# A state-space scan's forward pass, taken apart into steps, with the tensor engine's order through it written by hand

## The chip, the cores and the metric

The kernel runs on one core of one Trainium2 chip. The metric is the device time in microseconds (us) of one execution. TensorE (PE) does matrix products, VectorE (DVE), ScalarE (ACT) and GpSimd (POOL) do the elementwise work, SyncE (SP) issues nearly all transfers (DMA).

## The reference, cut to what matters

Two layers run over 1024 latent and 256 context tokens (1280 in all) with 1024 channels. The change lies in the even layer: a bidirectional state-space scan (16 heads of 64 channels in 2 groups, state of 128, chunks of 128 tokens) beside a convolution branch, and one output projection over both. For one direction the reference computes

```python
def ssd_chunked(x, dt, a, bm, cm, h0):
    ...
    y_diag = jnp.einsum('btlgn,btsgn,btlsgr->...', cc, bc, decay) @ xdt   # within a chunk
    states = jnp.einsum('btsgn,btsgr,btsgrp->btgrpn', bc, decay_to_end, xdt)
    ...  # h_in: state entering each chunk, by a scan over chunks
    y_off = jnp.einsum('btlgn,btgrpn,btlgr->btlgrp', cc, h_in, jnp.exp(a_cum))
    return y_diag + y_off
```

(the first line is drawn together from two). Both directions are summed with a skip term, gated by silu(z), normalised (RMS) and give the scan's half of the concatenation that the output projection `w_out` multiplies. The other half, the convolution's, is multiplied by the lower half of `w_out`.

## The kernel before

Before the stage of the change, the input projections, the convolution branch and the backward pass over the states (`ssd_back`) are done, and their results lie in DRAM. The stage (in `layer0`, inside `with ExitStack() as e3`) does three things side by side over ten chunks, or token tiles, of 128 tokens:

- The scan, class `SsdFwd`, one object `S[c]` for each chunk. `prep` loads the chunk (`xt`, `bcT`, the rows `rst` that `rows` is cast from), scales x on POOL (`tmp`, L1488), makes the forward state `Hf` for the next chunk (two products, L1495, each in a bank `ms`, added on DVE at L1499), the product of C and B (L1508) and the diagonal's coefficients. `mix` makes the output in four quarters (g, j) of four heads each: two products with 15 rows give the exponents (L1553, banks `sg0` and `sg1`, called the pair below), DVE merges them (L1556), ACT takes the exponential (`dec`, L1558), POOL multiplies by C^T B (L1559), and 8 small products of two records each (L1563) add up the diagonal part in bank `yd`. The parts that come from the states entering the chunk are four products, one for each group and direction (L1542, bank `m2`), each scaled and added on DVE (L1545, L1546). `finish` gates with z (L1570), takes the RMS statistic and transposes (L1578) into `wt_d`.
- `stage_b`, for each token tile the convolution's half of the output projection: 48 products (L1009) of 512 columns in two banks `m0` and `m1`, called the filler below, with their input loaded and split (`yl`, L997, L157, L158), then a gate and the residual (L1042, L1043).
- 16 columns of the next layer's modulation (`mod_chan`, L207 to L213): for each, two halves of weights (`mr`, one buffer, L1134) are loaded, cast on ACT and split on DVE (`mh`, `ml`, two buffers), multiplied in 16 small products, copied, and turned by a last product (L212). They use the banks of the filler (`mm`).

Nothing in this stage is ordered by hand: the program's order gives priorities, and the framework's scheduler orders each engine's instructions ahead of the run by its own estimate of times. On the chip each engine follows that order. Behind the stage, `stage_a` multiplies the scan's half by the upper half of `w_out` (also L1009), with weights split into the buffers of the lower half (L961, L962). The attention of the second layer already runs in a block whose TensorE order is written by hand.

Two banks carry the tag `ms`: states, C^T B, transposes and row broadcasts share them.

Of the kernel before, what the change touches and what calls it, by code (L numbers as in the profile page):

```python
# [7 lines left out]
F32 = mybir.dt.float32  # L8
# [81 lines left out]
def run(steps):  # L90
    """Emit a sequence that is emitted in steps."""
    for _ in steps:
        pass
# [6 lines left out]
# What is done on the tensor engine beside the attention, in this order: projections of queries (q) and gates (g) of a group's  # L100
# two head pairs, both halves of the output projection by token tile (c, d) and their weights (R, W, V); @n: from the n-th unit on.
# [4 lines left out]
# Columns of it for each key tile, by unit of the attention.  # L106
BESIDE = (2944,) * 10 + (3840,) * 6


class Kern:  # L110
# [78 lines left out]
    def mod_chan_(self, layer, m, dst, pool, plus=0.0, halves=1, bank="mm", ahead=None, raw=None, parts=None):  # L189
        """Columns m*128.. of the modulation, channel-major [P, 2] (latents, context)."""  # L190
# [24 lines left out]
    def gate_rows(self, layer, j, dst, bank="ms"):  # L215
        """Gate of one stream broadcast over partitions, [P, D]."""
# [8 lines left out]
    def layer0(self):  # L225
# [63 lines left out]
        with ExitStack() as e3:  # L289
# [12 lines left out]
            self.stage_b(2, ob, w, yb_d, tb_d, grow, y0)  # L302
            S[0].prep()
            for c in range(NT):
                S[c].mix()
                if c < NT - 1:
                    S[c + 1].prep()
                S[c].finish()
                if c < NT - 1:
                    self.stage_b((c + 3) % NT, ob, w, yb_d, tb_d, grow)  # L310
                for _ in range(2):
                    if mods:
                        m, d, plus = mods.pop(0)
                        self.mod_chan(1, m, d, mp, plus=plus, halves=2, ahead=ahead)
                        if not mods:
                            em.close()
                            wl3 = ea.enter_context(self.pool(name="wl3", bufs=1))
                            for k in range(4, 6):
                                wa.append((k, wl3.tile([P, D], F32, name=f"wa{k}", tag=f"wa{k}"), (wl3, f"wa{k}")))
                                nc.sync.dma_start(wa[k][1], A["wout0"][k])  # L320
                if c == 4:
                    for k in range(4):
                        nc.vector.tensor_copy(wa[k][1][:1, :1], self.Hf[:1, :1])
                        nc.sync.dma_start(wa[k][1], A["wout0"][k])
# [42 lines left out]
    def layer1(self, h1, va_d, e0, free_h1):  # L367
# [56 lines left out]
    def rope(self, q, ps, a, b, out):  # L424
        """Rotated queries or keys of two heads (128 channels), latents a..b."""
# [65 lines left out]
    def attention(self, wp, W, hhi, hlo, kf_d, va_d, yc_d, gd_d, yd_d, den_d, rd_d, sk_d, ew, free_h1):  # L491
        tc, nc, A = self.tc, self.nc, self.A
        LS = SLICES[:2]
        with ExitStack() as e:
# [44 lines left out]
            def fill(kv):  # L539
                """Stationary forms of one group's keys and values."""  # L540
# [20 lines left out]
            def rest():  # L561
                """What fills the tensor engine beside the attention, with the columns of each step; None while there is nothing to do."""
# [98 lines left out]
    def att_max(self, kv, s, qf, KV, out, u, sk_d):  # L661
        """Stationary-side queries of 2 blocks and the shift of each row."""
# [58 lines left out]
    def att_s(self, KV, mv, b, x, kb, off):  # L721
        """Exponentials of the scores of one key tile, 4 heads, split."""
# [32 lines left out]
    def out1_open(self, yc_d, wr, raws):  # L755
        """Pools and first half of the last output weight."""
# [9 lines left out]
    def out1_c(self, o, t):  # L766
        """The latent stream's residual plus the gated-MLP half of the output projection."""
# [15 lines left out]
    def out1_den(self, q, den_d, rd_d, sk_d, s, h0=0, h1=16):  # L783
        """Reciprocals of twice the softmax denominators, sinks included, of a quarter of the queries, heads h0..h1."""
# [12 lines left out]
    def out1_next(self, o, qp, wr):  # L797
        """Second half of the last output weight."""
# [10 lines left out]
    def out1_y(self, o, q, yd_d, gd_d, rd_d, t0, n, k0, k1, eng):  # L809
        """Gated attention of tokens t0..t0+n (within a quarter), channel tiles k0..k1, split."""  # L810
# [23 lines left out]
    def out1_mm(self, ps, y, w, f, ks, a=0, i0=0):  # L834
        """Channel tiles ks of the product for one half of the channels."""
# [7 lines left out]
    def out1_ln(self, o, x, ps, t):  # L843
        """Residual and the last layer norm."""
# [23 lines left out]
    def out1_d(self, o, q, ten, t, y0):  # L868
        """The attention's half of the output projection of one token tile."""
# [15 lines left out]
    def out1_d67(self, o, q, ten):  # L885
        """The last quarter: the last group's channels come last."""
# [20 lines left out]
    def conformer(self, cv, csum, e):  # L907
        """silu(layer norm over channels) of the convolution, in place."""
# [38 lines left out]
    def split_wo(self, wo, raws, slots, vec=None):  # L947
        """Split one half of an output weight; low parts go to free slots and to those of the values loaded for the tiles before."""
# [17 lines left out]
    def load_wo(self, wo, wr, src, pool_lo=(), more=(), raws=()):  # L966
        """One half (8 K tiles) of an output weight, split; raws are loaded already, the next ones land in the slots of more."""
# [19 lines left out]
    def out_mm(self, ob, src, w, parts=None, by_k=False):  # L987
        """Token tile of an output projection half: two PSUM banks."""
# [23 lines left out]
    def ln_mv(self, q, t):  # L1012
        """mean and rstd over the free dimension."""
# [586 lines left out]
```

## Time and profile before

| | us |
|---|---|
| median of 3 runs | 2266.37 |
| lowest and highest | 2262.7 and 2266.95 |
| span of the profiled execution | 2267.6 |
| PE busy in it | 2148.1 (95%) |
| DVE / ACT / POOL busy | 1470.1 / 1005.1 / 1015.7 |

For the profiled execution no other time than its span is given. The span is read from the first to the last instruction. A matmul's end is modelled, so that a busy PE is not one at its peak; gaps between starts tell more. PEclk is the granted clock as a share of 2.4 GHz; 0.5 is the lower of its two levels, 1.2 GHz. A matmul of plain 32-bit operands leaves two records in the trace.

### The profile page before, as it was taken

The numbers are of one execution on the slowest core, as the hardware profiler recorded it, in microseconds if no ns is written. First come the engines' busy times: TensorE is split into PE (matmuls) and PEld (weight loads), VectorE is DVE, ScalarE is ACT, GpSimd is POOL, SyncE is SP. The second block draws the span as 40 slices with busy tenths as digits, with TensorE's granted clock in tenths as the row PEclk, the third lists the DMA queues.
The fourth block names the chain that finished last, engine by engine and source line by source line (L and its number), as shares of the span: only waits on it lengthen the run. The fifth ranks groups of instructions, "written<-read, shape, count | busy, mean of one in ns | idle before, by whom it ended". The sixth has DMA issues, their size and how long they took to land.

```text
span 2267.6 us, 28582 instructions
## 1 busy us (share of the span) xinstructions
PE 2148.1 (95%) x10748; PEld 1647.3 (73%) x10748; DVE 1470.1 (65%) x1912; ACT 1005.1 (44%) x1553; POOL 1015.7 (45%) x652
## 2 busy tenths in 40 slices
PE   7998998889999999999999999999999999899997
PEld 6877876769997766656789788888666666666676
DVE  6799999988743377677775133223665566566677
ACT  4355565543552233333333233325556666545510
POOL 0088998870223355444330128433344444424453
PEclk9999999989999999899999999999999999899998
DMA  7121111115535765555434224323112111523363
GB/s 271 57 67 57 42 51 64 63 59 170 180 113 191 249 194 176 169 192 180 140 115 134 75 77 170 128 84 98 51 45 60 31 45 53 161 83 116 111 187 128
DMA packets 160145, 262.79 MB, mean 116 GB/s; under 512 B 19028, under 2 KB 98768, under 8 KB 159752
## 3 DMA queue, kind: packets, MB, share of 16 engines
q1 hardware_dynamic: 158584, 257.45, 34.9%
q0 software_dynamic: 1280, 3.26, 0.5%
q8 instruction: 84, 1.38, 0.2%
q14 instruction: 53, 0.43, 0.1%
q10 hardware_dynamic: 144, 0.26, 0.0%
HBM read 186.55 MB, written 74.32 MB: 115 GB/s over the span
## 4 chain that ended last, share of the span: by engine, by line
PE 58%; DVE 7%; DMA 5%; ACT 3%; issue 2%; POOL 2%; SPq 0%; POOLq 0%; DVEq 0%; ACTq 0%
PE m L170 28%; PE m L1009 12%; PE po L746 4%; PE st L728 2%; PE st L729 1%; PE ms L691 1%; DMA mr<-in_modw_dram 1%; PE m L840 1%; PE po L1542 1%; DVE ml L158 1%; PE ms L686 1%; ACT rb L433 1%; POOL ks L828 1%; PE m L691 1%; PE yd L1563 1%
## 5 line engine op out<-in xcount | busy, mean ns | idle before, releaser
L170 PE MATMUL m<-hhi,wh 128*128 128x512 f32 (+1 forms) x840 | 306.9, 369 | 36.8 <-ACT pad L1235 35.2
L1216 POOL TENSOR_TENSOR accq<-accq,prod 128x1295 f32<-128x1295 f32 x90 | 319.0, 3545 | 43.7 <-ACT prod L1215 30.3
L170 PE MATMUL m<-hlo,wh 128*128 128x512 f32 (+1 forms) x840 | 308.2, 367 | 0.0
L170 PE MATMUL m<-hhi,wl 128*128 128x512 f32 (+1 forms) x840 | 306.1, 365 | 1.0 <-DVE wl L158 1.0
L1224 DVE SCALAR_TENSOR_TENSOR acc<-u,vwh,acc 128x1295 f32<-128x1295 f32 x150 | 234.8, 1565 | 6.1 <-issue 2.2
L739 POOL TENSOR_TENSOR pl<-pt,ph 128x512 fp32r<-128x512 f32 x96 | 129.0, 1344 | 236.7 <-ACT ph L738 227.7
L170 PE MATMUL m<-h1hi,wh 128*128 128x512 f32 (+1 forms) x544 | 218.3, 401 | 2.0 <-ACT rb L433 1.4
L170 PE MATMUL m<-h1lo,wh 128*128 128x512 f32 (+1 forms) x544 | 217.0, 399 | 0.0
L170 PE MATMUL m<-h1hi,wl 128*128 128x512 f32 (+1 forms) x544 | 216.3, 398 | 0.0
L170 PEld LDWEIGHTS m<-hhi,wh 128*128 128x128 f32 x840 | 161.7, 194 | 64.4 <-ACT pad L1235 38.3
L1009 PE MATMUL m<-woh,yh 128*128 128x512 f32 x448 | 187.0, 421 | 0.6 <-ACT yh L157 0.2
L1009 PE MATMUL m<-wol,yh 128*128 128x512 f32 x448 | 185.3, 414 | 1.0 <-DVE wol L158 0.5
L1009 PE MATMUL m<-woh,ylo 128*128 128x512 f32 x448 | 185.0, 413 | 0.5 <-DVE ylo L158 0.5
L170 PEld LDWEIGHTS m<-hhi,wl 128*128 128x128 f32 x840 | 162.6, 194 | 27.9 <-issue 3.4
L170 PEld LDWEIGHTS m<-hlo,wh 128*128 128x128 f32 x840 | 163.0, 194 | 24.6 <-issue 2.4
L1215 ACT ACTIVATE prod<-u,vwh 128x1295 f32<-128x1295 f32 x90 | 123.4, 1378 | 82.0 <-POOL accq L1216 81.9
L738 ACT CAST ph<-pt 128x512 fp32r<-128x512 f32 x152 | 93.1, 619 | 115.3 <-PE po L746 107.9
L158 POOL TENSOR_TENSOR wl<-wr,wh 128x1024 fp32r<-128x1024 f32 x33 | 80.6, 2443 | 122.7 <-ACT wh L157 99.0
L1244 DVE SCALAR_TENSOR_TENSOR acc<-pad,vecs,acc 128x1282 f32<-128x1282 f32 x48 | 131.8, 2748 | 3.2 <-issue 1.8
L170 PEld LDWEIGHTS m<-h1hi,wh 128*128 128x128 f32 x544 | 103.2, 190 | 28.7 <-issue 2.6
L746 PE MATMUL po<-ph,vs 128*66 128x512 f32 x304 | 122.9, 404 | 0.8 <-ACT ph L738 0.8
L731 ACT ACTIVATE pt<-st 128x512 f32<-128x512 f32 x152 | 90.7, 597 | 74.2 <-PE st L729 54.5
(360 smaller groups left out, 4890.2 us busy)
## 6 DMA issues: line engine op xcount, KB each, us to landing
wr<-in_wch_dram SPq DMA_DIRECT2D x69, 512.0 KB
mr<-in_modw_dram SPq DMA_DIRECT2D x64, 256.0 KB
mr<-in_modw_dram SPq DMA_DIRECT2D x16, 512.0 KB
wor<-in_wout_dram SPq DMA_DIRECT2D x16, 512.0 KB
xcT<-xbc_d SPq DMA_DIRECT2D x20, 320.0 KB
xt_d<-xtok SPq DMA_DIRECT2D x20, 320.0 KB
xtok<-xt_d SPq DMA_DIRECT2D x10, 640.0 KB
xt<-xt_d SPq DMA_DIRECT2D x10, 640.0 KB
```

The costliest lines, as they stand in the source:

```text
L158: (nc.gpsimd if pool_lo else nc.vector).tensor_tensor(lo, src, hi.bitcast(F32), op=ALU.subtract)
L170: nc.tensor.matmul(out, x(k), y(k), start=(c == 0), stop=(c == tot - 1))
L691: nc.tensor.matmul(ps[:, :nw], mv1[0:64, b, h], ks1[0:64, C + w0 * P:C + w0 * P + nw], start=True, stop=True)
L731: nc.scalar.activation(p.rearrange("p h t -> p (h t)"), ps, AF.Exp, scale=0.125)
L738: nc.scalar.copy(ph, p)
L739: (nc.gpsimd if x in (0, 1, 3) else nc.vector).tensor_tensor(pl, p, ph.bitcast(F32), op=ALU.subtract)
L746: nc.tensor.matmul(po[:66], vs[:, kb, v], p[y], start=first and i == 0, stop=last and i == 2)
L1009: nc.tensor.matmul(ps[f], y[u][:, k], w[k][v][:, 512 * f:512 * f + 512], start=i + j == 0, stop=i + j == 9)
L1215: nc.scalar.activation(pr, u[:, k:k + N], AF.Copy, scale=vwh[:, i, k:k + 1])
L1216: nc.gpsimd.tensor_tensor(acc, acc, pr, op=ALU.add)
L1224: nc.vector.scalar_tensor_tensor(acc[:, :N], u[:, k:k + N], vwh[:, i, k:k + 1], acc[:, :N], op0=ALU.mult, op1=ALU.add)
L1244: nc.vector.scalar_tensor_tensor(acc, pad[:, k:k + N], w(k), acc, op0=ALU.mult, op1=ALU.add)
```

## The change

The scan's three methods become eight steps (`load`, `states`, `cbt`, `begin`, `seg`, `off`, `diag`, `gate`, `turn`, and `load_z`), and the loop over chunks becomes one over 41 quarters `n`, with chunk `c` and quarter `z`. Inside a block the order of TensorE's instructions is the program's; the other engines and the queues are ordered by the scheduler as before. In each quarter come the pair of quarter n, filler, one product with an entering state, filler, the diagonal products of quarter n-1, then (by z) the transposes of the chunk before, C^T B or the states of the chunk after, and filler. `rest` is the filler: the 48 products of each tile with two modulations at fixed places among them; `beside` takes as many columns of it as it is given, 6900 in a quarter. All that lies before the first quarter is the first chunk's `states`, 8192 columns of filler, its `cbt`, and 4096 columns. Modulations move from the filler's banks to `ms`; the next tile's input is asked for behind the 7th product of a tile; the entering states have two buffers in place of one, `t3` alternates with a second buffer, the scaled x has one of its own from the second chunk on, `dec` has two in place of three. In the diff, comments and lines that are moved as they are have been left out.

```diff
--- before.py
+++ after.py
...
+SSD_BESIDE = 6900
...
             S = [SsdFwd(self, c, xbc_d, xt_d, hb_d, zs_d, wt_d, rstd, q) for c in range(NT)]
-            self.stage_b(2, ob, w, yb_d, tb_d, grow, y0)
-            S[0].prep()
-            for c in range(NT):
-                S[c].mix()
-                if c < NT - 1:
-                    S[c + 1].prep()
-                S[c].finish()
-                if c < NT - 1:
-                    self.stage_b((c + 3) % NT, ob, w, yb_d, tb_d, grow)
-                for _ in range(2):
-                    if mods:
-                        m, d, plus = mods.pop(0)
-                        self.mod_chan(1, m, d, mp, plus=plus, halves=2, ahead=ahead)
...
+            def rest():
+                tiles = (*range(2, NT), 0, 1)
+                y = y0
+                for i, t in enumerate(tiles):
+                    ps = [self.bank("mm") for _ in range(2)]
+                    mod = None
+                    for n, cols in enumerate(self.out_mm_(ps, y, w, i == 0)):
+                        yield cols
+                        if n == 6 and i < NT - 1:
+                            y_next = self.stage_b_y(tiles[i + 1], ob, yb_d)
+                        if n in (8, 27) and mods:
+                            m, d, plus = mods.pop(0)
+                            mod = self.mod_chan_(1, m, d, mp, plus=plus, halves=2, bank="ms", ahead=ahead)
+                            yield next(mod)
+                        if n in (14, 33) and mod:
+                            next(mod)
+                        if n in (22, 41) and mod:
+                            run(mod)
+                            mod = None
+                            yield 256
...
+                    self.stage_b_end(t, ob, ps, tb_d, grow)
+                    y = y_next
+            def beside(cols):
+                hold[0] += cols
+                while hold[0] > 0:
+                    c = next(oth, None)
...
+                    hold[0] -= c
+            with tc.manual_schedule(engines={mybir.EngineType.PE}):
+                oth = rest()
+                S[0].load()
+                S[0].states()
+                beside(8192)
+                S[0].cbt()
+                nc.scalar.copy(self.rows, self.rst)
+                beside(4096)
+                for n in range(4 * NT + 1):
+                    c, z = divmod(n, 4)
+                    if c < NT:
+                        if z == 0:
+                            S[c].begin()
+                        S[c].seg(z // 2, z % 2)
+                    beside(SSD_BESIDE * 0.35)
+                    if c < NT:
+                        S[c].off(z // 2, 1 - z % 2)
+                    beside(SSD_BESIDE * 0.3)
+                    if n:
+                        S[(n - 1) // 4].diag((n - 1) % 4 // 2, (n - 1) % 2)
+                        if z == 0:
+                            S[c - 1].gate()
+                    if z == 1:
+                        if c:
+                            S[c - 1].turn()
+                        S[c].load_z()
+                    if c < NT - 1:
+                        if z == 1:
+                            S[c + 1].load()
+                        elif z == 2:
+                            S[c + 1].cbt()
+                        elif z == 3:
+                            nc.scalar.copy(self.rows, self.rst)
+                            S[c + 1].states()
...
+                    beside(SSD_BESIDE * 0.35)
+                beside(4096)
+                S[NT - 1].turn()
+                run(oth)
...
 class SsdFwd:
...
-    def prep(self):
+    def load(self):
...
+            xs = self.xs = K.we.tile([P, D], F32, name="xsf", tag="ylo0") if c else q.tile([P, D], F32, name="tmp", bufs=1)
...
+    def states(self):
...
+            nc.tensor.matmul(ps, xt[:, D + g * P:D + (g + 1) * P], self.xs[:, cs], start=True, stop=True)
...
+    def cbt(self):
...
-        junk = q.tile([P, 512], F32, name="dec", bufs=3)[:, :P]
+        junk = q.tile([P, P], F32, name="junk", bufs=1)
...
-    def mix(self):
+    def begin(self):
+        t3 = self.t3 = K.we.tile([P, D], F32, name="t3", tag="yh0") if c % 2 else q.tile([P, D], F32, name="t3", bufs=1)
...
+                hb = q.tile([P, 512], F32, name="hbt", bufs=2)
...
+    def load_z(self):
+    def seg(self, g, j):
...
+        M = self.M[g, j] = q.tile([P, 4, P], F32, name="dec")
...
+    def off(self, g, d):
...
+        po = K.pp.tile([P, 512], F32, name="po", tag="m2", bufs=1)
...
+    def diag(self, g, j):
...
-    def finish(self):
+    def gate(self):
...
+    def turn(self):
```

## Rows read from the trace of the kernel before

**Rows 1.** The page's head: span and instructions

```profile
span 2267.6 us, 28582 instructions
```

**Rows 2.** Windows: stretch, length, busy us of five engines (counts), PEclk, DMA share, GB/s

```profile
784.20:1102.30 318.10, 299.38 (x1817) 194.90 (x1816) 242.48 (x362) 108.97 (x165) 154.58 (x100) 0.94 0.53 177
...
832.20:839.10 6.90, 6.90 (x30) 5.12 (x30) 3.89 (x6) 2.25 (x4) 5.43 (x3) 0.51 0.65 193
```

**Rows 3.** PE groups by line, 784.2 to 1102.3: busy, mean ns, idle before

```profile
L1009 PE MATMUL m<-woh,yh 128*128 128x512 f32 x184 | 79.6, 440 | 0.4 <-DVE mod L213 0.2 <-DVE t L1545 0.2
...
L1009 PE MATMUL m<-woh,ylo 128*128 128x512 f32 x181 | 76.6, 423 | 0.0
```

**Rows 4.** Waits of PE, 784.2 to 1102.3: total us, times, longest

```profile
PE po L1542 <- DVE t L1545: 5.8, 7, 1.8
PE m L207 <- DVE ml L158: 4.1, 5, 1.3
...
PE ms L1508 <- DVE Hf L1499: 1.2, 1, 1.2
...
PE m L1009 <- DVE t L1545: 0.2, 1, 0.2
```

**Rows 5.** Windows, one of the stretches that hold PE's waits

```profile
888.00:894.00 6.00, 3.81 (x30) 2.35 (x28) 6.00 (x7) 2.23 (x4) 5.72 (x4) 0.97 0.59 200
```

**Rows 6.** Timeline of PE: start, us, line, product, count

```profile
1060.71 0.50 PE L1553 MATMUL sg<-rows 15*128 15x512 f32 x1
1061.14 0.50 PE L1009 MATMUL m<-woh,yh 128*128 128x512 f32 x1
1061.48 0.39 PE L1009 MATMUL m<-wol,yh 128*128 128x512 f32 x1
...
1088.07 0.39 PE L1009 MATMUL m<-woh,yh 128*128 128x512 f32 x1
1088.38 0.50 PE L1553 MATMUL sg<-rows 15*128 15x512 f32 x2
1088.82 0.50 PE L1009 MATMUL m<-wol,yh 128*128 128x512 f32 x1
1089.15 0.40 PE L1009 MATMUL m<-woh,ylo 128*128 128x512 f32 x1
1089.38 0.40 PE L1009 MATMUL m<-woh,yh 128*128 128x512 f32 x1
```

**Rows 7.** Timelines of SP's queue, POOL, PE and DVE around the stage's start

```profile
787.74 0.89 SPq L1483 DMA_DIRECT2D xt<-xt_d  x1
...
795.16 2.59 POOL L1488 TENSOR_TENSOR tmp<-xt,wst 128x1024 f32<-128x1024 f32 x1 [7.19 <-DMA xt<-xt_d]
...
784.20 2.88 PE L221 MATMUL ms<-cs,gcol 128*128 128x128 f32 x24
...
797.80 1.12 PE L1495 MATMUL ms<-tmp,xt 128*128 128x512 f32 x2 [1.53 <-POOL tmp L1488]
...
803.12 0.69 DVE L158 TENSOR_TENSOR ml<-mr,mh 128x512 fp32r<-128x512 f32 x1 [0.89 <-ACT mh L157]
```

**Rows 8.** One half of modulation weights in three timelines; last, the tile's casts

```profile
854.50 0.22 PE L207 MATMUL m<-mh,scond 128*4 128x128 f32 x1
...
859.47 0.38 SPq L1134 DMA_DIRECT2D mr<-in_modw_dram  x1
...
865.07 0.69 DVE L158 TENSOR_TENSOR ml<-mr,mh 128x512 fp32r<-128x512 f32 x1 [2.78 <-ACT mh L157]
...
L157 ACT CAST mh<-mr x31: 608/618/641, 802.5 to 1048.3; 128x512 fp32r<-128x512 f32 x31
```

**Rows 9.** The last chunk: PE's transposes, and POOL's share of a quarter

```profile
1101.28 1.03 PE L1578 MATMUL ms<-cs,zst 128*128 128x128 f32 x8
...
L1559 POOL TENSOR_TENSOR dec<-dec,cbs 128x512 f32<-128x512 f32 x40 | 58.1, 1455 | 72.2 <-ACT dec L1558 68.5 <-DMA mr<-in_modw_dram 3.4
```

More of the change, by code (lines that the diff above doesn't have):

```diff
@@ new lines, in layer0 @@
+            hold = [0]
+            def rest():
[18 more added lines that the diff above has]
+                            yield 256
+                            if not mods:
+                                em.close()
+                                wl3 = ea.enter_context(self.pool(name="wl3", bufs=1))
+                                for k in range(4, 6):
+                                    wa.append((k, wl3.tile([P, D], F32, name=f"wa{k}", tag=f"wa{k}"), (wl3, f"wa{k}")))
+                                    nc.sync.dma_start(wa[k][1], A["wout0"][k])
+                    self.stage_b_end(t, ob, ps, tb_d, grow)
+                    y = y_next
@@ L1325, in inproj0 @@
                 nc.sync.dma_start(wb[n - 1][1], A["wout0"][8 + n])
[L1326 removed]
+        we = self.we = ewl.enter_context(self.pool(name="we", bufs=1, side="right"))
         y = wl.tile([P, 8, P], F32, name="yl0", tag="wb0")
@@ L1475, in __init__ @@
         self.rstd = rstd
-    def prep(self):
+    def load(self):
         K, c, q, nc = self.K, self.c, self.q, self.K.nc
         xbc_d, xt_d = self.d[:2]
-        H = self.H = K.Hf if c else None
         xt = self.xt = q.tile([P, 10 * P], F32, name="xt2")
@@ L1485, in prep @@
         nc.sync.dma_start(bc, xbc_d[8:12, :, c * P:(c + 1) * P].rearrange("k p t -> p k t"))
-        if c < NT - 1:
-            xs = q.tile([P, D], F32, name="tmp", bufs=1)
-            nc.gpsimd.tensor_tensor(h16(xs), h16(xt[:, :D]), K.wst[:, 0, c].unsqueeze(2).broadcast_to([P, 16, 64]), op=ALU.mult)
-            H2 = K.Hf = q.tile([P, D], F32, name="Hf")
-            if H is not None:
-                nc.gpsimd.tensor_tensor(h16(H2), h16(H), K.expS[:, 0, c].unsqueeze(2).broadcast_to([P, 16, 64]), op=ALU.mult)
-            for g in range(2):
-                cs = slice(512 * g, 512 * g + 512)
-                ps = K.bank("ms")
-                nc.tensor.matmul(ps, xt[:, D + g * P:D + (g + 1) * P], xs[:, cs], start=True, stop=True)
-                if H is None:
-                    nc.vector.tensor_copy(H2[:, cs], ps)
-                else:
-                    nc.vector.tensor_tensor(H2[:, cs], H2[:, cs], ps, op=ALU.add)
         for g in range(2):
@@ L1504, in prep @@
                 nc.sync.dma_start(K.rst[z:z + 12, 1024:].rearrange("k (a l) -> k a l", a=2), K.rB_d[d, c].rearrange("t (q g a) l -> (t q) g a l", q=4, g=2)[:, g])
-        nc.scalar.copy(K.rows, K.rst)
+        if c < NT - 1:
+            xs = self.xs = K.we.tile([P, D], F32, name="xsf", tag="ylo0") if c else q.tile([P, D], F32, name="tmp", bufs=1)
+            nc.gpsimd.tensor_tensor(h16(xs), h16(xt[:, :D]), K.wst[:, 0, c].unsqueeze(2).broadcast_to([P, 16, 64]), op=ALU.mult)
+    def states(self):
+        K, c, q, nc = self.K, self.c, self.q, self.K.nc
+        H, xt = K.Hf if c else None, self.xt
+        self.H = H
+        if c == NT - 1:
+            return
+        H2 = K.Hf = q.tile([P, D], F32, name="Hf")
+        if H is not None:
+            nc.gpsimd.tensor_tensor(h16(H2), h16(H), K.expS[:, 0, c].unsqueeze(2).broadcast_to([P, 16, 64]), op=ALU.mult)
+        for g in range(2):
+            cs = slice(512 * g, 512 * g + 512)
+            ps = K.bank("ms")
+            nc.tensor.matmul(ps, xt[:, D + g * P:D + (g + 1) * P], self.xs[:, cs], start=True, stop=True)
+            if H is None:
+                nc.vector.tensor_copy(H2[:, cs], ps)
+            else:
+                nc.vector.tensor_tensor(H2[:, cs], H2[:, cs], ps, op=ALU.add)
+    def cbt(self):
+        K, c, q, nc = self.K, self.c, self.q, self.K.nc
+        bc = self.bc
         ps = K.bank("ms")
@@ new lines, in off @@
+    def off(self, g, d):
+        K, c, q, nc = self.K, self.c, self.q, self.K.nc
+        cs = slice(512 * g, 512 * g + 512)
+        if d:
+            S = self.hb[g] if self.hb else None
+        else:
+            S = self.H[:, cs] if self.H is not None else None
+        if S is None:
+            return
+        po = K.pp.tile([P, 512], F32, name="po", tag="m2", bufs=1)
+        nc.tensor.matmul(po, self.bc[:, 2 + g], S, start=True, stop=True)
+        ea = K.expA[:, d, c, 8 * g:8 * g + 8].unsqueeze(2).broadcast_to([P, 8, 64])
+        t2 = q.tile([P, 512], F32, name="t2", bufs=1)
+        nc.vector.tensor_tensor(h16(t2), h16(po), ea, op=ALU.mult)
+        nc.vector.tensor_tensor(self.t3[:, cs], self.t3[:, cs], t2, op=ALU.add)
@@ new lines, in diag @@
+    def diag(self, g, j):
+        K, nc = self.K, self.K.nc
+        if j == 0:
+            self.yd = K.px.tile([P, 512], F32, name="yd", tag="yd", bufs=1)
+        yd, M = self.yd, self.M.pop((g, j))
+        for h in range(4):
+            o = 256 * j + 64 * h
+            for f in range(2):
+                nc.tensor.matmul(yd[64 * f:64 * f + 64, o:o + 64], M[:, h, 64 * f:64 * f + 64], self.xt[:, 512 * g + o:512 * g + o + 64], start=True, stop=True)
+        if j:
+            cs = slice(512 * g, 512 * g + 512)
+            nc.vector.tensor_tensor(self.t3[:, cs], yd, self.t3[:, cs], op=ALU.add)
```

96 lines of the change are left out of this document (37 added, 59 removed).

## The prediction

> **What bounds the kernel now.** I read the page's head first: TensorE is by far the busiest engine, and the span is 2267.6 us [rows 1]. Since a busy share is an average, the stage that the change touches has to be read by itself: it runs from 784.2 us, the last product of the gates' projections, to 1102.3, the end of the last chunk's transposes. The windows give for it 318.1 us, with TensorE busy for 299.4, VectorE for 242.5, GpSimd for 154.6, and a granted clock of 0.94 [rows 2]. So TensorE bounds it and nothing else comes near, but three sorts of time can still be won.
>
> First the waits: the thirteen lines of TensorE's waits sum to 18.3 us, from 5.8 for the entering states' bank down to 0.2 [rows 4]. Second the clock: 0.94 over 318.1 us is 0.06 x 318.1 = 19.1 us lost at the lower level; one of the five stretches is 832.2 to 839.1, at 0.51 [rows 2]. They follow bunches of waits: from 888 to 894 TensorE is busy for 3.81 of 6 us while VectorE is busy for all of it and GpSimd for 5.72 [rows 5]; behind it the clock falls. Third the order: of the 40 pairs, 21 stand apart, as at 1060.71; 19 stand together, as at 1088.38 [rows 6].
>
> The stage already does part of its successor's work: three groups of L1009 hold 184, 182 and 181 products [rows 3], 547 where `stage_b` has 480. Two starts in a run of them are 0.23 us apart (1089.15, 1089.38) [rows 6], so 67 x 0.23 = 15.4 us belong to `stage_a`, and the stage's own time is 318.1 - 15.4 = 302.7 us. Without waits and clock, 302.7 - 18.3 - 19.1 = 265.3 us of products and changes between kinds remain. This is what the new order starts from.
>
> **The products themselves.** None is removed or added; the order changes. A pair kept together, from 1088.07 to 1089.15, costs 1.08 - 2 x 0.23 = 0.62 us; a single one takes 0.43 until the next product and makes that one 0.34 instead of 0.23 long [rows 6]. So the 21 pairs now split cost 0.43 to 0.62 more each; at 0.5 the gain is 10.5 us. Against it, the new order sets each pair, each product with a state and each diagonal group singly between filler, where before they often stand beside each other; each change back to filler costs 0.11 (0.34 against 0.23) [rows 6]. Of some 110 such groups about half had a neighbour: 5 us. New sum: 265.3 - 10.5 + 5 = 259.8 (bounds 253 to 266).
>
> **The start.** In program order the block's first TensorE instruction is the first chunk's `states`, which needs the scaled x. Before, GpSimd starts that at 795.16, having waited 7.19 us for the load issued at 787.74, and the product goes at 797.80 [rows 7]; 48 filler products were run ahead of 805.8. Now no filler may pass it. The load itself may come some 4 us earlier, since fewer transfers stand before it, but the first modulation sits behind nine filler products and needs its second half of weights, split at 803.12 + 0.69 = 803.8 [rows 7], behind a VectorE queue that the change doesn't shorten. From there the first pair is 13 filler products (3.0), `cbt` and half a modulation (1.0) away: 807.8. Of the 23.6 us since 784.2, TensorE works for 22 x 0.23 = 5.1 plus some 7 for row broadcasts (2.88 for the first 24 [rows 7]), states, modulation and `cbt`: 11.7 us are idle (bounds 6, if both come early, to 14).
>
> **The quarters.** The filler has 480 x 512 columns plus 16 x 1280 for modulations, 266,240; 12,288 go ahead of the first quarter, and 6900 in each make it last for 36.8 quarters. In these, seven places could wait. (1) The pair's exponents: merge, exponential and GpSimd's product (1.46 us [rows 9]) have a quarter and more, about 8 us of TensorE's work, before the diagonal needs them; they wait only behind a bunch. (2) The bank of the entering states, today's largest wait at 5.8 us [rows 4], is asked for once in a quarter instead of twice in a row: gone. (3) `states` needs two `ms` banks. By the order as written, a modulation holds one of the two between its first and last product, and this falls on six of the nine `states` (chunks 1 to 6): the second product waits for VectorE to empty the first one's bank. Today's wait for just that is 1.2 us [rows 4]; taken at 1.0, 6 us (bounds 4 to 14). The transposes fall outside. (4) Modulation weights: raw has one buffer, so a mod's second half is loaded only after the first is split. From the products that free the buffers to the second half ready, as from 854.50 over the issue at 859.47 to 865.07 + 0.69, took 11.3 us [rows 8]; ten such stretches, the last from 1039.85, took 7.9 to 17.7, mean 11.2. The new places are 19 and 29 filler products apart, of 48 in a tile of 259.8 / 10 = 26 us: 10.3 and 15.7 us, the short one usually with a `states` wait, 11.5. The ten stretches exceed 11.5 by 0.85 on the mean, 6.8 us for eight short spacings; as the products of one modulation now stand together (here they begin at 854.50 and go on in pieces), I take 4 (bounds 0 to 8 x 6.2 = 50). (5) The next tile's input is asked for 41 products ahead, about 22 us against the few that load, cast and split take: nothing; if SP's queue, which is in order, held it back, a tile would lose what is late. (6) On SP's queue the chunk's loads move ahead by half a chunk and z's load behind the transposes, three quarters (some 19 us) before its use; their bytes stay the same. GpSimd's scaling of x gets its own buffer, two quarters ahead. Both nothing. (7) `dec` with two buffers is exactly enough. For all bunches that remain: 2 us (bounds 0 to 10).
>
> **The tail.** From quarter 37 on there is no filler. Three quarters of pair, state and diagonal products take about 5.3 us with the transposes of chunk 8; from the last pair to the last transposes the chain of merge, exponential, GpSimd's 1.46 [rows 9], diagonal, add and gate adds at least 6.5; the same way takes 12.9 today, 1088.38 to 1101.28 [rows 6, 9], among the split of the next weights. I take 14.7 in all with 0.9 for the transposes; 9 are work, 6 idle (bounds 3 to 10). Products of `stage_a` might fill some of it.
>
> **The clock.** Today the lower level follows bunches of waits as that of 888 us [rows 5], and the quarters leave single ones of 1 or 2 us; I expect it only at the tail, where quarters run without filler, and once more: 4 us (bounds 0 to 31, below).
>
> A rule speaks against the change here. The Trainium skill, "TensorE: Matmul & The Clock Gate", section "A second HAM failure mode: psum-queue depth-cycling", says that many very short idle times between groups of matmuls are enough to make the clock swing between its levels. The trace agrees so far: 18.3 us of waits, none over 1.8, stand beside 19.1 lost [rows 2, 4]. By that rule my waits would cost as much again.
>
> **Sum.** 259.8 + 11.7 + 6 (states) + 4 (weights) + 2 + 6 (tail) + 4 (clock) = 293.5 us against 302.7: 9.2 less. The span becomes 2258.4. The only time given for the profiled execution is its span, 1.2 over the median of 2266.37, so the forecast is 2257 us.
>
> **Rivals.** *Even spread.* What makes today's waits is VectorE's and GpSimd's bunches [rows 5]; VectorE has 242.5 us of work [rows 2], under nine tenths of what is left, and the quarters spread it. Then waits and clock loss vanish but for 3 us of `states`, start and tail cost 6 and 3: 259.8 + 12 = 271.8, 31 less: 2236 us. A fifth.
>
> *Eaten at both ends.* Start 14 and tail 10 instead of 11.7 and 6: 299.8, 2.9 less: 2263, no change within the measurement. For it speaks that both ends run without filler. A fifth.
>
> *The weights' chain bounds* (slower). 31 casts lie between 802.5 and 1048.3, 8.2 us each [rows 8], so 16.4 for a modulation. Today TensorE's own pace explains this. If it is the chain's pace (loads late on SP's queue, VectorE's split late), a short spacing waits 16.4 - 11.5 = 4.9 and a long one 0.7: 8 x 4.9 + 7 x 0.7 = 44 instead of 4, which is 31 slower: 2297. It decides from a mean of 13.2 us on: then each short spacing waits 1.7, 13.2 in all, which is my 4 and the gain of 9.2. Chance 0.09.
>
> *The clock follows every wait* (slower). 29.7 us of waits, start and tail, each losing 19.1 / 18.3 of itself again, are 31 instead of 4: 18 slower, 2284. It decides where more than 13 us are lost. It is what the rule named above would do. Chance 0.08.
>
> **Chances.** A measurement here tells about 0.2%, 4.5 us, from no change. Forecast, 4.5 to 18 us faster: 0.43. Even spread: 0.2. Both ends: 0.2. Slower ones: 0.17. The range runs from the even spread, 2236, to 2280, below the two slow cases' full price.
>
> **What would show it.** Right: pairs in one row of the timeline; waits of the entering states' bank gone; filler missing ahead of the first `states`; TensorE's waits led by L1495's bank and by L207. Wrong: clock 0.94 or less over the stage, waits of L207 over 15 us, or diagonal products waiting for GpSimd.

## The result and the profile after

The changed kernel takes 2282.57 us (median of 4 runs, 2281.9 to 2287.45) against 2264.53 for the kernel before on the same chip: ratio 1.0088, 95% interval 1.006 to 1.0116. It is 0.9% slower, and outside the range given. The profiled execution is 13.2 us longer than that of before [rows 1]. The head of its page:

```profile
span 2280.8 us, 28602 instructions
```

The window of its stage (columns as in [rows 2]), from the same start to the end of the last chunk's transposes:

```profile
784.20:1116.30 332.10, 297.58 (x1828) 195.12 (x1828) 241.85 (x362) 110.36 (x165) 153.33 (x101) 0.91 0.51 170
```

The granted clock is 0.91 where before it was 0.94 [rows 2], so up to 0.09 x 332.1 = 29.9 us are lost at the lower level; a part of that time TensorE was waiting anyway, and the table below takes it out. TensorE's waits in the stage (total, times, longest), to be set beside [rows 4]:

```profile
PE ms L1571 <- DVE Hf L1575: 17.2, 6, 4.1
PE ms L223 <- ACT g L225: 5.9, 1, 5.9
PE ms L209 <- ACT mh L159: 4.4, 1, 4.4
PE ms L1571 <- POOL tmp L1556: 2.7, 1, 2.7
PE ms L209 <- DVE Hf L1575: 1.7, 1, 1.7
PE ms L1676 <- DVE zst L1663: 1.7, 1, 1.7
PE ms L209 <- DVE ml L160: 0.8, 1, 0.8
```

They sum to 34.4 us instead of 18.3. The wait for the entering states' bank is gone, as forecast; half of the new sum is one line. L1571 is the product of `states`, and the six waits are those of its second product, at chunks 1 to 6. One of them in the timeline (start, us, engine, line; in brackets the wait and what ended it):

```profile
899.38 1.13 PE L1571 MATMUL ms<-xsf,xt 128*128 128x512 f32 x2
...
903.35 2.06 PE L1571 MATMUL ms<-xsf,xt 128*128 128x512 f32 x2 [2.84 <-DVE Hf L1575]
...
898.58 2.35 POOL L1567 TENSOR_TENSOR Hf<-Hf,expS 128x1024 f32<-128x1024 f32 x1
...
900.91 1.79 DVE L160 TENSOR_TENSOR ml<-mr,mh 128x512 fp32r<-128x512 f32 x1 [1.74 <-ACT mh L159]
902.62 0.68 DVE L1575 TENSOR_TENSOR Hf<-Hf,ms 128x512 f32<-128x512 f32 x1
...
900.26 0.62 ACT L159 CAST mh<-mr 128x512 fp32r<-128x512 f32 x1 [2.74 <-DMA mr<-in_modw_dram]
```

The first product is done at 900.5. The add that empties its bank (L1575) starts only at 902.62. Two things stand before it. GpSimd scales the state until 900.93. And VectorE has the subtraction of a modulation weight (L160) ahead of the add in its queue; that takes 1.79 us, after a wait of 1.74 for ScalarE's cast, which had itself waited 2.74 for the load of the weights. It is so in all six: the subtraction is the last thing ahead of the add, it waited 0.2 to 2.1 us for the cast, the cast 1.1 to 3.3 for the load, and GpSimd's scaling was done before the subtraction each time. Then the second product may start. Behind it, the clock is at its lower level (1.2 GHz) over the 3.4 us of this line:

```profile
903.40:906.80 3.40, 3.40 (x7) 1.70 (x7) 0.69 (x1) 0.00 (x0) 0.00 (x0) 0.50 0.29 88
```

For all kernels below I split the stretch from the first row broadcast (L223; L221 before) to the first product of the function `gmlp`, some 270 us behind the stage (L525; L463 before), which holds exactly 3141 TensorE records in every one of them. *Idle* is the time in which none of them runs, *half clock* the time that the granted-clock records give at the lower level, *of it idle* the part of that in which none runs, and which therefore loses nothing to the clock. *Rest* is the length less idle less half of the half clock that isn't idle: what the products and the changes between them cost. These are worked out from one profiled execution of each kernel, and outside the stretch these executions differ by 12 us (1673.2 to 1685.1), so that single us in a column say little; medians and ratios are from all runs, the ratio against the kernel before on the same chip.

| Kernel | median us | ratio to before (95%) | length | idle | half clock | of it idle | rest |
|---|---|---|---|---|---|---|---|
| before | 2264.53 |  | 588.5 | 21.7 | 41.0 | 0.5 | 546.6 |
| after | 2282.57 | 1.0088 (1.006 to 1.0116) | 600.3 | 37.6 | 58.0 | 8.0 | 537.6 |
| e1_bank | 2251.05 | 0.9931 (0.991 to 0.9952) | 576.2 | 22.6 | 41.0 | 7.4 | 536.7 |
| e3_early | 2254.26 | 0.9951 (0.9933 to 0.9969) | 577.4 | 26.1 | 30.7 | 5.8 | 538.8 |
| e4_release | 2280.74 | 1.0063 (1.0039 to 1.0087) | 594.0 | 35.5 | 44.4 | 6.8 | 539.7 |
| e10_pool | 2264.27 | 0.9996 (0.9979 to 1.0013) | 579.5 | 31.8 | 23.9 | 7.4 | 539.4 |
| e6_before_ms | 2270.85 | 1.0025 (1.0007 to 1.0043) | 592.0 | 21.3 | 47.8 | 1.6 | 547.6 |
| e8_apart | 2265.89 | 1.0011 (0.9991 to 1.0031) | 586.3 | 19.3 | 23.9 | 7.0 | 558.5 |
| e11_group | 2266.75 | 0.9993 (0.9977 to 1.001) | 585.1 | 36.5 | 27.3 | 8.9 | 539.4 |
| e2_start | 2284.82 | 1.0084 (1.0054 to 1.0114) | 602.2 | 39.4 | 61.4 | 11.2 | 537.6 |
| e7_later | 2249.76 | 0.9938 (0.9913 to 0.9963) | 570.6 | 23.2 | 20.5 | 3.8 | 539.1 |
| e9_start | 2251.01 | 0.994 (0.992 to 0.996) | 568.8 | 22.8 | 10.2 | 0.4 | 541.1 |
| e13_bankpool | 2252.5 | 0.9949 (0.9932 to 0.9966) | 572.3 | 22.4 | 27.3 | 4.7 | 538.6 |
| e12_all | 2257.01 | 0.9961 (0.9943 to 0.9979) | 579.3 | 26.9 | 27.3 | 0.0 | 538.7 |

Rest depends on the order almost alone: 547 to 548 in both kernels with the scheduler's order, 537 to 541 in the written one, 559 with the pairs taken apart.

### The profile page after: what moved, and what is told of

Same layout as the page of the kernel before. It is cut to its first block, busy times and chain, and to the rows that moved or that the text cites. A ratio compares the mean times of both kernels' runs of the same rounds, so it can differ in the third digit from the quotient of the medians.

```text
span 2280.8 us, 28602 instructions
## 1 busy us (share of the span) xinstructions
PE 2146.5 (94%) x10748; PEld 1648.0 (72%) x10748; DVE 1456.9 (64%) x1912; ACT 1006.2 (44%) x1553; POOL 1014.5 (44%) x652
## 4 chain that ended last, share of the span: by engine, by line
PE 60%; DVE 5%; DMA 5%; ACT 4%; issue 3%; POOL 2%; SPq 0%; POOLq 0%; DVEq 0%; ACTq 0%
PE m L172 27%; PE m L1071 13%; PE po L808 4%; PE st L790 2%; PE st L791 1%; PE ms L753 1%; DMA mr<-in_modw_dram 1%; PE po L1639 1%; PE m L902 1%; PE ms L209 1%; PE ms L748 1%; PE ms L1571 1%; PE yd L1654 1%; ACT mv L734 1%; PE m L753 1%
## 5 line engine op out<-in xcount | busy, mean ns | idle before, releaser
L172 PEld LDWEIGHTS m<-hhi,wh 128*128 128x128 f32 x840 | 163.0, 196 | 63.1 <-ACT pad L1299 36.5
L1071 PE MATMUL m<-woh,yh 128*128 128x512 f32 x448 | 193.3, 432 | 0.2 <-ACT yh L159 0.2
L1071 PE MATMUL m<-woh,ylo 128*128 128x512 f32 x448 | 191.0, 426 | 0.5 <-DVE ylo L160 0.5
L1071 PE MATMUL m<-wol,yh 128*128 128x512 f32 x448 | 190.2, 425 | 0.0
L160 POOL TENSOR_TENSOR wl<-wr,wh 128x1024 fp32r<-128x1024 f32 x33 | 81.5, 2470 | 123.0 <-ACT wh L159 98.8
```

The source lines that it names most:

```text
L160: (nc.gpsimd if pool_lo else nc.vector).tensor_tensor(lo, src, hi.bitcast(F32), op=ALU.subtract)
L172: nc.tensor.matmul(out, x(k), y(k), start=(c == 0), stop=(c == tot - 1))
L1071: nc.tensor.matmul(ps[f], y[u][:, k], w[k][v][:, 512 * f:512 * f + 512], start=i + j == 0, stop=i + j == 9)
```

## The experiments

**The second `states` product in another bank** (the kernel after, one line):

```diff
-            ps = K.bank("ms")
+            ps = K.pp.tile([P, 512], F32, name="po", tag="m2", bufs=1) if g else K.bank("ms")
```

> The changed kernel, but the second product of each `states` step goes to the bank of the entering states (m2) instead of `ms`; nothing else. Theory (bank): in the changed kernel six of these products wait 17.2 us in all for VectorE's add into the state, because a modulation holds one of the two `ms` banks, and TensorE's clock is at its lower level for 30.6 us behind five of them, 15.3 lost. With a bank of their own they do not wait: 32 us less, 2250. Rival (bunch): VectorE and GpSimd are late in any case, the wait comes back at the next product that needs them (entering state, diagonal), and the time stays at 2277 to 2283.

2251.05 us, 31.5 less than the kernel after and now faster than before. The line of six waits is gone; what stands at the head is the start. First lines of its waits:

```profile
PE ms L209 <- ACT mh L159: 6.3, 1, 6.3
PE ms L223 <- ACT g L225: 5.9, 1, 5.9
PE ms L1571 <- POOL tmp L1556: 2.7, 1, 2.7
```

Against the kernel after, idle falls by 15.0, the loss to the clock by 8.2 (from 25.0 to 16.8) and rest by 0.9: together the 24.1 by which the stretch is shorter. So the one shared bank costs both, the waits and the clock behind them. Against the kernel before, idle is the same within 1 us, the clock takes 3.4 less (16.8 for 20.2), and most of the gain is rest, 9.9 us.

**The modulation a little earlier in its tile**, so that the held bank no longer meets `states`:

```diff
-                        if n in (8, 27) and mods:
+                        if n in (0, 27) and mods:
...
-                        if n in (14, 33) and mod:
+                        if n in (6, 33) and mod:
...
-                        if n in (22, 41) and mod:
+                        if n in (14, 41) and mod:
```

> The changed kernel, but a tile's first modulation has its steps behind products 0, 6 and 14 instead of 8, 14 and 22, so that by the order as written it holds no `ms` bank when `states` comes; banks and `states` stay as they are. Theory (bank): the six waits vanish with their clock loss, 2250, as if the products had a bank of their own; the spacing of the modulations becomes 27 and 21 products, so the weights' wait may cost or give 3 us. Rival (bunch): waits of the same size come back elsewhere, 2277 to 2283.

2254.26 us. Without any touch to `states` the six waits and most of the loss are gone too, which a cause inside `states` (the scaled state, the loads of x) could not explain. The edit also takes the weights' split away from the add, so it shows the meeting as the cause; that the bank is what makes TensorE wait in it, e1_bank shows. What remains of the meeting is the modulation's own wait for the bank:

```profile
PE ms L209 <- DVE Hf L1575: 5.9, 4, 1.8
```

**The forward state's products a quarter earlier**, so that GpSimd gets the state's buffer and can scale it before the first `states` product is done:

```diff
-                        S[c].off(z // 2, 1 - z % 2)
+                        S[c].off(z // 2, int(z in (0, 3)))
```

> The changed kernel, but the four entering-state products of a chunk take backward, forward, forward, backward instead of backward, forward, backward, forward, so that the forward state is read for the last time a quarter earlier and GpSimd may scale it for the next chunk that much earlier. Theory (bank, emptied late because GpSimd's scaling of 1.9 to 2.4 us can start only behind the chunk's last product with the old state): each of the six waits falls from 2.9 us to 1 to 2, 6 to 11 us less with up to as much again in clock: 2262 to 2275. Rival (VectorE's own queue is what is late, here the split of modulation weights): the waits stay at 17 us, 2280 to 2285.

2280.74 us: hardly better, the rival's time. The waits only fall from 17.2 to 14.4. VectorE's timeline at one of them, whose second product goes at 897.45:

```profile
893.23 1.89 DVE L1643 TENSOR_TENSOR t<-t,t 128x512 f32<-128x512 f32 x1
895.05 1.75 DVE L160 TENSOR_TENSOR ml<-mr,mh 128x512 fp32r<-128x512 f32 x1
896.72 0.68 DVE L1575 TENSOR_TENSOR Hf<-Hf,ms 128x512 f32<-128x512 f32 x1
```

The first product starts at 893.72 and is done some 1.1 later; the add stands behind 1.89 and 1.75 us of other work in an engine that takes its queue in order. GpSimd had been done with the scaling since 890.87. So the scaling was not what the add waited for last; VectorE's queue was.

**The same, with the weights' low part subtracted on GpSimd**, which takes L160, and its wait for the cast and the load, out of VectorE's queue:

```diff
-        return self.load_w(pool, self.A["modw"][layer, i // 2][:, 4 * (i % 2):4 * (i % 2) + 4], [P, 4, P], "m", prio=prio)
+        return self.load_w(pool, self.A["modw"][layer, i // 2][:, 4 * (i % 2):4 * (i % 2) + 4], [P, 4, P], "m", pool_lo=layer == 1, prio=prio)
```

> The kernel after with two of its causes for a late bank taken away, while both `states` products stay in the modulation's pair of banks: the forward states' products go one quarter earlier (the run before it with that alone stood at 2281), and the low part of the modulation weights is subtracted on GpSimd instead of VectorE. Theory A (the six `states` waits are long because VectorE has a weight split, 0.67 to 1.75 us, and an add of 1.3 to 1.9 us queued ahead of the add that empties the bank): the waits fall from 14.4 to 6 to 10 us and some of the half clock goes, 2264 to 2274. Rival B (they are long because of the chain itself or of GpSimd, and a busier GpSimd makes it no better): the waits stay at 13 us or more, 2276 to 2288.

2264.27 us, theory A. The line of the six waits is now

```profile
PE ms L1571 <- DVE Hf L1575: 9.2, 6, 2.7
```

and VectorE's timeline at the same place has the add right behind its other work; the second product goes at 896.73, after 1.57 us:

```profile
894.79 1.29 DVE L1643 TENSOR_TENSOR t<-t,t 128x512 f32<-128x512 f32 x1
896.00 0.68 DVE L1575 TENSOR_TENSOR Hf<-Hf,ms 128x512 f32<-128x512 f32 x1
```

Six waits of 0.8 to 2.7 us, and behind none of them a stretch at the lower clock begins: half clock falls to 23.9. The subtraction was not moved alone. In the kernel after, GpSimd's scaling ended up to 2.9 us behind the first product, so it would have been the next link.

**The bank alone, in the kernel before** (its order is still the scheduler's):

```diff
-                        self.mod_chan(1, m, d, mp, plus=plus, halves=2, ahead=ahead)
+                        self.mod_chan(1, m, d, mp, plus=plus, halves=2, bank="ms", ahead=ahead)
```

> The kernel before, with one word changed: its modulations take their bank from the states' pair of banks, as in the kernel after. Theory A (the bank costs time where the order is written by hand; an order found by a scheduler that sees the banks puts other work between the two products of `states`): within 5 us of 2265. Rival B (the bank alone is the price, whatever the order): 2265 plus the 27 that the kernel after lost by it, 2285 to 2292, with a sum of waits before the `states` products near 17 us.

2270.85 us, 0.25% over before and just outside A's 5 us, far from B's 2285. Idle is the same (21.3); its largest line is no longer than

```profile
PE po L1542 <- DVE t L1545: 3.5, 3, 2.5
```

and a second `states` product waits for 0.3 us there at most. The scheduler's order puts other work between: in seven chunks a modulation holds a bank when the first product comes, and the second then comes 15 to 45 TensorE records later. So the price belongs to the bank together with an order that cannot give way. The stretch is 3.5 us longer, 2.9 of it by the longer half clock; why that came isn't settled.

**The pairs taken apart again** (on e1_bank):

```diff
+            def one():
+                hold[0] -= next(oth, 0)
...
             seg.append(sg)
+            if d == 0:
+                between()
```

> The kernel after with the second `states` product in its own bank (2251), and one filler product put between the two products of each 15-row pair, 37 pairs or so; nothing else moves. Theory A (two such products run side by side when they are next to each other, as the prediction took it, 0.43 to 0.62 us a pair): 2251 + 37 x 0.5 = 2269, 2265 to 2274. Rival B (the gain of the hand-written order lies elsewhere, and a pair taken apart costs one more change of kind, 0.11 us): 2251 + 4 = 2255.

2265.89 us, theory A. Rest rises by 21.8 us for 36 pairs taken apart (four at the end have no filler left): 0.61 each. (The stretch is only 10.1 longer, since in this execution idle and clock took 3.3 and 8.3 less.) One in the timeline:

```profile
1001.35 0.50 PE L1623 MATMUL sg<-rows 15*128 15x512 f32 x1
1001.77 0.50 PE L1074 MATMUL m<-wol,yh 128*128 128x512 f32 x1
1002.21 0.50 PE L1623 MATMUL sg<-rows 15*128 15x512 f32 x1
1002.63 0.50 PE L1074 MATMUL m<-woh,ylo 128*128 128x512 f32 x1
```

The 21 pairs that were apart before, at 0.61, make 12.8 us: more than the 9.0 between the rest of before and of after. So the written order gains by the pairs and gives back 3.8 elsewhere.

**A quarter's groups side by side** (on e1_bank): filler no longer between pair, state product and diagonal, but behind them all.

```diff
                         S[c].seg(z // 2, z % 2)
-                    beside(SSD_BESIDE * 0.35)
...
-                    beside(SSD_BESIDE * 0.3)
...
-                            S[c + 1].states()
...
-                    beside(SSD_BESIDE * 0.35)
+                    beside(SSD_BESIDE * 0.5)
+                    if z == 3 and c < NT - 1:
+                        S[c + 1].states()
+                    beside(SSD_BESIDE * 0.5)
```

> The kernel after with the second `states` product in its own bank (2251), and a quarter's pair, state product and diagonal products set side by side with the filler behind them, instead of filler between each; `states` goes into the middle of that filler. Theory A (each return to filler costs 0.11 us, as the prediction's term of +5 us had it): some 70 returns less, 7.7 us, 2241 to 2246. Rival B (a return costs nothing that adds up, since the products beside each other overlap no better): 2249 to 2253. Rival C (transposes and state products now come right behind the work that they need; waits of 0.5 to 2 us at a third of the 41 quarters): 2256 to 2270.

2266.75 us, the time of theory C: the second half of the transposes now waits for ScalarE to copy the first half.

```profile
PE ms L1676 <- ACT tmp L1677: 12.8, 7, 4.1
```

The reason is the shared pair of banks again, at another place. One of the seven, with the modulation's products (L209, and L214 as its last) around it:

```profile
904.87 0.40 PE L209 MATMUL ms<-ml,scond 128*4 128x128 f32 x4
...
909.20 0.66 PE L1676 MATMUL ms<-cs,zst 128*128 128x128 f32 x4
911.28 0.66 PE L1676 MATMUL ms<-cs,zst 128*128 128x128 f32 x4 [1.42 <-ACT tmp L1677]
...
913.25 0.38 PE L214 MATMUL ms<-vecs,modrow 4*128 4x2 f32 x2
```

In all seven a modulation holds the other bank; the three chunks whose transposes meet none do not wait, and neither in the kernel after nor in e1_bank does any transpose meet one. The rest, where A wanted 7.7 us less, is 2.7 more than e1_bank's: setting the groups side by side saves nothing.

**The start.** Three runs: filler ahead of the first `states` (on the kernel after); modulations only from the filler's second tile on (on e1_bank); and both, with filler ahead of the second row broadcasts too.

```diff
                 S[0].load()
-                S[0].states()
                 beside(8192)
+                S[0].states()
```

> The changed kernel, but the first 8192 columns of filler stand ahead of the first chunk's `states` instead of behind it. Theory (start): the two waits at the start (5.9 us for the row broadcasts' bank, 2.7 for the scaled x) are filled, the first low stretch of the clock (13.7 us, 6.8 lost) goes, at most 15 less; the modulation among this filler still waits for its weights until about 804 us, which takes back some: 2268 to 2275. The `states` waits stay at about 17 us. Rival (start is set by loads): the first pair waits for its rows in any case and starts no earlier than 806: 2279 to 2283.

```diff
-                        if n in (8, 27) and mods:
+                        if i and n in (8, 27) and mods:
```

> The kernel after with the second `states` product in its own bank (2251), and the modulations in tiles 1 to 8 of the filler instead of 0 to 7. Theory A (the first tile's modulations come before their weights are split, 6.3 + 0.8 us of waits with a stretch of half clock behind them): 5 to 9 us less, 2242 to 2246. Rival B (the start as a whole is set by loads, and another wait takes their place; or the later end of the modulations delays what follows the stage): 2249 to 2253.

```diff
-        self.gate_rows(0, 1, g1)
...
                 S[0].load()
-                S[0].states()
-                beside(8192)
+                beside(4096)
+                self.gate_rows(0, 1, g1)
+                beside(4096)
+                S[0].states()
```

> As the run with modulations in tiles 1 to 8, and at the start eight filler products ahead of the second stream's row broadcasts and eight more between these and the first `states`. Theory A (without a modulation among them those 16 products fill the 5.9 us wait for ScalarE's copy of the row broadcasts and the 2.7 us wait for the scaled x): 3 to 7 us below the run with modulations in tiles 1 to 8. Rival B (the filler's own weights and the first chunk's loads set the start): within 2 us of that run.

The first gives 2284.82, no gain, and above the rival's 2279 to 2283. Its wait for the row broadcasts' copy halves, but the modulation behind the filler then waits for its weights:

```profile
PE ms L209 <- DVE ml L160: 6.5, 2, 3.7
PE ms L209 <- ACT mh L159: 5.2, 2, 4.4
PE ms L223 <- ACT g L225: 2.8, 1, 2.8
```

The loads and splits set the start, not the filler's place. The other two give 2249.76 and 2251.01: rival B for both. In the profiled executions half clock falls to 20.5 and 10.2 and the stretch is 5.6 and 7.4 us shorter than e1_bank's, yet their ratios to before are 0.9938 and 0.994, against its 0.9931, each with 0.2 to 0.25% on either side. Outside the stretch those two executions took 8.1 and 5.2 us more than that of e1_bank. A gain of that size cannot be told from none here. Later modulations also pay it back in part: in the last run they wait 6.7 us for VectorE's half of their weights.

**All together.** e1_bank with e10_pool's two edits, and all five edits:

> The kernel after with the second `states` product in its own bank (2251), with the forward states' products one quarter earlier and the low part of the modulation weights subtracted on GpSimd. Theory A (the six waits are gone already, so a shorter VectorE queue has nothing more to give): 2248 to 2254. Rival B (VectorE's queue also delays what is left, waits of 0.4 to 0.8 us and their stretches of half clock): 2240 to 2247.

> All edits together: the second `states` product in its own bank, modulations in tiles 1 to 8, sixteen filler products at the start among the second row broadcasts and ahead of the first `states`, the forward states' products one quarter earlier, the low part of the modulation weights on GpSimd. Its sum of waits would be some 12 us, 19.7 with the bank alone less the start's 8.6 and with 1 to 2 us of small ones, and the half clock 10 to 20 us instead of 37.5. Theory A (the stage's gain is the program's): 2237 to 2245. Rival B (as in the two runs with the later modulations, the stage's gain is not found in the program's time): 2247 to 2252.

2252.5 us (theory A) and 2257.01 us (neither: above both). With all five, the weights that GpSimd now splits come late for the later modulations:

```profile
PE ms L209 <- POOL ml L160: 12.4, 8, 3.4
```

The bank alone, one line, has the lowest ratio that was run, 0.9931 of before; nothing added to it showed more.

## Why the prediction was wrong

Its sum and what the stretch shows, as differences to before:

| Term | forecast us | measured us |
|---|---|---|
| products and changes | -10.5 + 5 = -5.5 | 537.6 - 546.6 = -9.0 |
| waits | 29.7 - 18.3 = +11.4 | 37.6 - 21.7 = +15.9 |
| clock | 4 - 19.1 = -15.1 | 25.0 - 20.2 = +4.8 |
| sum | -9.2 | +11.7 (length: +11.8) |

**The clock is the step that failed.** The prediction said that the quarters leave single waits of 1 or 2 us, and that the lower level would come only at the tail and once more: 4 us. It came eight times in the stage: twice at the start (13.7 us from 790.8, 10.2 from 818.1), once at the tail (3.4 from 1094.5), and behind five of the six `states` waits, 30.6 us at half clock in all, 15.3 lost. With the 9.7 of the start and the tail that makes 25.0 us.

**The price of a `states` wait was mis-sized**, place (3) of the quarters. The mechanism, the number of six and the chunks were right. But 17.2 us came instead of 6, beyond the bound of 14. The 1.0 apiece was taken from a single wait of before, the 1.2 of [rows 4], with no look at what had stood ahead of the add there. The queues of the other engines should have been asked: who is ahead of that add in VectorE's queue, what does that wait for, and what must GpSimd finish first? Easing GpSimd's scaling alone left 14.4 us (e4_release), taking the subtraction out of VectorE's queue as well left 9.2 (e10_pool). e1_bank and e3_early show that without the meeting the waits and the loss behind them go.

The other terms of the waits came out near or better. The first pair goes at 810.25 instead of 807.8; the start's waits, the weights' among them, are 5.9 + 4.4 + 2.7 + 0.8 = 13.8, against 11.7 (by its own terms 11.5: 23.6 less 5.1 and 7) and 4 for the weights in all. The tail waits 1.7 instead of 6, since products of `stage_a` do fill it, as the prediction left open. Weights' chain: its rival is refuted, with 5.2 us of TensorE's waits for casts and splits, all at the start. But the chain came in by another way, which the prediction hadn't: the split, waiting for cast and load, stood ahead of the emptying add.

**The products** gained more than said. The pairs' 10.5 was somewhat low (12.8 by the price of e8_apart). Of that, 3.8 are given back, close to the +5 for lone groups; but e11_group, which puts them side by side, doesn't win them back, so that what the 3.8 belong to isn't shown.

**Of the rivals**, "the clock follows every wait" gave 2284 and the runs 2282.57. The number fits and the direction too, but not its rule of as much lost as waited: the loss to the clock over idle is 0.67 in the kernel after, 0.26 in e10_pool and 0.22 in e9_start. That its number fits is luck in part: the idle time came out longer than its waits (37.6 for 29.7), the loss to the clock smaller (25.0 for 31), the products shorter. The rule of the Trainium skill behind it ("TensorE: Matmul & The Clock Gate", section "A second HAM failure mode: psum-queue depth-cycling") speaks of very short idle times between groups of matmuls. Here single waits hurt: five of six waits of 2.4 to 4.1 us were followed by the lower level, none of six of 0.8 to 2.7 in e10_pool. Length alone doesn't decide. In e10_pool one of 2.7 was not followed by it, in the kernel after those of 2.6 and 2.8 were; and in e3_early two waits of the modulation for the bank, 1.8 and 1.6 us, were followed by it too. What decides stays open.

**Of the signs named**, pairs in one row (all 40), the entering states' waits gone and filler missing ahead of the first `states` came, as did L1571 (L1495 before) and L209 (L207) at the head of the waits; and so did the sign against it, a clock below 0.94. The first pair:

```profile
810.25 0.50 PE L1620 MATMUL sg<-rows 15*128 15x512 f32 x2
```

## What to carry to other kernels

Where an order is written by hand, list for each bank who holds it at every step; two products that need both banks of a pair, while a third party sits on one, wait for the whole chain that empties the first. Price such a wait by what is queued on the emptying engine at that time, and by what that work waits for, not by the shortest wait of its kind, and allow for the clock behind it. A change of the order asks for the list anew: e11_group moved the same meeting from `states` to the transposes. And measure the order by itself: with the bank apart it made the stretch 12 us shorter than before, hidden under a loss of 24 that one bank made and one line takes away.

## What the runs showed of the hardware

**Two 15-row products on different rows run side by side.** Next to each other they start within 0.01 us and take 0.44 us to the next product's start (1088.38 to 1088.82 [rows 6]), one alone 0.42 (1001.35 to 1001.77 above); taken apart, a pair cost 0.61 us more (e8_apart).

**VectorE slows down beside GpSimd, by where its inputs lie.** Two operations of the kernel after, each 36 times on 128 x 512 elements (min/median/max ns):

```profile
L1643 DVE TENSOR_TENSOR t<-t,t x36: 679/1298/2431, 814.4 to 1105.8; 128x512 f32<-128x512 f32 x36
...
L1642 DVE TENSOR_TENSOR t<-po,expA x36: 677/691/693, 813.6 to 1103.5; 128x512 f32<-128x512 f32 x36
```

L1643 has both inputs in SBUF and L1642 one in PSUM. In the trace the eight of L1643 with no GpSimd work beside them take 0.68 to 0.69 us; of the 24 that run beside GpSimd for over half of their time, the median is 1.47. L1642 takes 0.69 in either case. The subtraction ahead of the emptying add is of the first kind: 0.67 us at 895.20 with no GpSimd work beside it, 1.79 at 900.91 with GpSimd at work for 1.26 of them. The Trainium skill ("SBUF — State Buffer", section "Who interferes with whom") says so: a VectorE instruction with two SBUF inputs contends with GpSimd's reads, one with at most one doesn't. The trace agrees, and this is a part of why the bank came free so late.
